# One transpose instruction per slab instead of two, in a kernel that rotates images

## Chip, cores, metric

The kernel runs on one core of a Trainium2 chip. The metric is device time in microseconds (us).

## The reference

```python
x = np.random.randn(32, 3, 256, 256).astype(np.float32)

def reference(x):
    return np.rot90(x, k=-1, axes=(-2, -1)).astype(np.float32)
```

It is a rotation of 96 planes by 90 degrees. Nothing is computed: 25.17 MB are read, 25.17 MB are written.

## The kernel before

The input is cut into 24 slabs of 1 MB. In a slab, each of 128 partitions holds 8 rows of 256 numbers. A load brings the slab in (issued on the SyncE queue), VectorE transposes it, and a store takes it out (issued on the ScalarE queue).

```python
R = 8
n_slabs = B * C * G // P            # 24
PARTS = 2
SHORT = 2
CP = R // PARTS
# ... cut: the views ld_v and st_v, 128 partitions x 2048 numbers per slab
in_pool = ctx.enter_context(tc.tile_pool(name="in_pool", bufs=12))
out_pool = ctx.enter_context(tc.tile_pool(name="out_pool", bufs=12))

for n in range(n_slabs):
    t_in = in_pool.tile([P, R * W], fp32, tag="t_in")
    nc.sync.dma_start(out=t_in, in_=ld_v[n])

    t_out = out_pool.tile([P, R * W], fp32, tag="t_out")
    src = t_in.rearrange("p (r g c) -> p c r g", r=R, c=R)
    dst = t_out.rearrange("p (c g r) -> p c r g", c=R, r=R)[:, :, ::-1, ::-1]
    for k in range(PARTS):
        cs = slice(k * CP, (k + 1) * CP)
        nc.vector.transpose(out=dst[:, cs], in_=src[:, cs])

    nc.scalar.dma_start(out=st_v[n], in_=t_out,
                        max_dma_last_dim=2048 if n < SHORT else 8192)
```

One store covers both halves of a slab, so it waits for both transposes (in the profile the second one of the first slab ends at 9.53 us and the first store is issued at 9.57 us). There are 12 buffers on each side, so loads can run far ahead.

## Time and profile before

| | before |
|---|---|
| time, median (lowest to highest) of the first 3 runs | 124.44 us (124.3 to 124.59) |
| span of the profiled run | 122.8 us |
| VectorE busy | 92.5 us, 75% |
| data moved, mean rate over the span | 50.34 MB, 410 GB/s |

The first page of the profile of the kernel before: the rows of busy tenths and of GB/s cut the span into 40 equal slices, and a 9 is 90% or more; DMA is the mean of the 16 DMA engines. The group line gives busy time, mean ns of one instruction and the idle time ahead of it.

```profile
span 122.8 us, 186 instructions
DVE 92.5 (75%) x48; POOL 0.2 (0%) x4
DVE  0199999999999999999999999897796693000000
...
DMA  3999999999999999999999999999999999999993
GB/s 93 422 427 427 393 427 422 415 420 432 426 408 411 427 427 427 427 427 427 427 427 430 427 427 427 427 427 430 427 430 427 427 427 430 424 427 427 427 430 163
...
q14 instruction: 1, 0.01, 0.0%
...
L54 DVE STREAM_TRANSPOSE t_out<-t_in 128x1024 f32<-128x1024 f32 x48 | 92.5, 2047 | 9.7 <-DMA t_in<-in_x_dram 7.9
```

The DVE row (VectorE) is full through the middle, and that alone would make VectorE look like the bound. The DMA row says more: it is full from the second slice to the last but one. So the DMA engines had transfers to work on all that time, even where VectorE was waiting or had finished.

The timeline of VectorE in the kernel before (start and duration in us; in brackets the idle time ahead and what ended it):

```profile
5.55 72.62 DVE L54 STREAM_TRANSPOSE t_out<-t_in 128x1024 f32<-128x1024 f32 x38 [5.55 <-DMA t_in<-in_x_dram]
78.62 3.98 DVE L54 STREAM_TRANSPOSE t_out<-t_in 128x1024 f32<-128x1024 f32 x2 [0.45 <-DMA t_in<-in_x_dram]
...
98.27 3.98 DVE L54 STREAM_TRANSPOSE t_out<-t_in 128x1024 f32<-128x1024 f32 x2 [0.97 <-DMA t_in<-in_x_dram]
```

VectorE is behind the loads until 78.17 us, with 38 transposes in one unbroken row. Then it has caught up and waits for each load. It ends at 98.27 + 3.98 = 102.25 us.

The windows view of the kernel before (busy time of VectorE and GpSimd, count of instructions, clock, share of the DMA engines' time, GB/s in each stretch of us):

```profile
12.00:42.00 30.00, 30.00 (x17) 0.00 (x0) 1.00 1.02 418
42.00:78.00 36.00, 36.00 (x19) 0.00 (x0) 1.00 1.01 427
78.00:102.00 24.00, 19.84 (x11) 0.00 (x0) 1.00 1.02 429
102.00:120.00 18.00, 0.25 (x1) 0.00 (x0) 1.00 1.01 425
120.00:123.00 3.00, 0.00 (x0) 0.00 (x0) 1.00 0.32 134
```

The rate is the same where VectorE is full (42 to 78 us), where it waits (78 to 102 us) and where it has nothing to do (102 to 120 us). In those last 18 us only stores move (the last packet of a load ends at 97.73 us): about seven slabs that VectorE had finished and that had been queueing, 18 us x 425 GB/s = 7.7 MB.

### The profile page before, as it was taken

What the parts mean: (1) busy time and instruction counts of PE and PEld (TensorE: products, weight loads), DVE (VectorE), ACT (ScalarE), POOL (GpSimd) and SP (SyncE); (2) the same over time, 40 slices, a digit from 0 to 9 for tenths busy, and PEclk for the clock granted to TensorE, in tenths of its full rate; (3) what the DMA queues carried; (4) which work ended last, traced back from release to release, by engine and by line L of the source; (5) the groups of instructions that cost most, each with busy time, mean ns of one, the idle gap of its engine ahead of it and who ended that gap; (6) DMA issues with size and microseconds to landing.
All of it is one profiled execution on the core that took longest, in us unless ns stands there. A gap on an engine that the chain in (4) does not pass through costs nothing.

```text
span 122.8 us, 186 instructions
## 1 busy us (share of the span) xinstructions
DVE 92.5 (75%) x48; POOL 0.2 (0%) x4
## 2 busy tenths in 40 slices
DVE  0199999999999999999999999897796693000000
POOL 0000000000000000000000000000000000000000
DMA  3999999999999999999999999999999999999993
GB/s 93 422 427 427 393 427 422 415 420 432 426 408 411 427 427 427 427 427 427 427 427 430 427 427 427 427 427 430 427 430 427 427 427 430 424 427 427 427 430 163
DMA packets 7681, 50.34 MB, mean 410 GB/s; under 512 B 768, under 2 KB 768, under 8 KB 1792
## 3 DMA queue, kind: packets, MB, share of 16 engines
q1 hardware_dynamic: 3456, 25.17, 49.3%
q10 hardware_dynamic: 4224, 25.17, 48.9%
q14 instruction: 1, 0.01, 0.0%
HBM read 25.17 MB, written 25.17 MB: 410 GB/s over the span
## 4 chain that ended last, share of the span: by engine, by line
DMA 72%; DVE 8%; DVEq 2%; SPq 1%; issue 0%
DMA t_in<-in_x_dram 72%; DVE t_out L54 8%; DVEq L83 2%; SPq L47 1%; DVEq L54 0%
## 5 line engine op out<-in xcount | busy, mean ns | idle before, releaser
L54 DVE STREAM_TRANSPOSE t_out<-t_in 128x1024 f32<-128x1024 f32 x48 | 92.5, 2047 | 9.7 <-DMA t_in<-in_x_dram 7.9
L72 POOL MEMSET const-bfloat16-1.0<- 128x1 bf16 x1 | 0.1, 101 | 0.0
L72 POOL MEMSET const-uint8-127<- 128x1 uint8 x1 | 0.1, 101 | 0.0
L72 POOL MEMSET const-float32-0.0<- 128x1 f32 x1 | 0.1, 98 | 0.2 <-issue 0.2
L72 POOL MEMSET const-float32-1.0<- 128x1 f32 x1 | 0.1, 98 | 0.0
## 6 DMA issues: line engine op xcount, KB each, us to landing
t_in<-in_x_dram SPq DMA_DIRECT2D x24, 1024.0 KB, 14.5
out_dram<-t_out ACTq DMA_DIRECT2D x24, 1024.0 KB, 19.5
```

The costliest lines, as they stand in the source:

```text
L47: nc.sync.dma_start(out=t_in, in_=ld_v[n])
L54: nc.vector.transpose(out=dst[:, cs], in_=src[:, cs])
L72: nc = _bacc.Bacc("TRN2", target_bir_lowering=False, num_devices=1)
L83: with _tile.TileContext(nc) as tc:
```

## The change

The intent: a slab needs only one transpose instruction, since its store waits for both halves anyway. The hope was that VectorE then pays once instead of twice for whatever an instruction costs beyond its elements; nothing had shown such a cost before the change (it came out at 0.06 us, below). The first and the last slab keep halves, where the pipeline fills and drains.

```diff
-    PARTS = 2
     SHORT = 2
-    CP = R // PARTS
 ...
-        for k in range(PARTS):
-            cs = slice(k * CP, (k + 1) * CP)
+        parts = 2 if n in (0, n_slabs - 1) else 1
+        for k in range(parts):
+            cs = slice(k * R // parts, (k + 1) * R // parts)
             nc.vector.transpose(out=dst[:, cs], in_=src[:, cs])
```

VectorE then has 26 instructions instead of 48: 22 of 2048 elements and 4 of 1024.

## The prediction

> What bounds the kernel now. The profile's first page gives a span of 122.8 us and 50.34 MB moved; the row of GB/s by slices lies at 408 to 432 from the second slice to the 39th, and the windows view gives a DMA share of 1.0 in every window from 3 us to 120 us. At 427 GB/s the bytes alone take 50.34 MB / 427 GB/s = 117.9 us; the rest of the span is about 2.5 us until the first load flows and about 2 us after the last bytes. The chain of waits that ended last is 72% DMA loads, 8% VectorE. [...] DMA bytes bind.
>
> VectorE is busy 75% (92.5 us). 38 transposes run without a break from 5.55 us to 78.17 us: 2.043 us each, started every (72.62 - 2.04) / 37 = 1.908 us, so each overlaps the next by 0.135 us. A slab costs VectorE 3.82 us, but DMA 2.1 MB / 427 GB/s = 4.9 us. From 78 us on VectorE waits for loads (gaps of 0.45 to 0.97 us per slab). Its last instruction ends at 102.25 us; DMA then still moves data at 427 GB/s until about 120.5 us, some 18 us of stores, about 7 to 8 slabs, queued behind. So the last transposes could come ten us later unseen.
>
> What the change does. It takes away 22 of 48 VectorE instructions (slabs 1 to 22 become one instruction of 2048 elements); elements, access patterns, loads, stores and buffers stay. A store already waited for both halves of its slab, and a load that takes a buffer over also waited for both, so nothing is released earlier or later by the merging itself. First and last slab are untouched. [...] Estimate from the trace: between nothing and 0.13 us is saved. I expect a duration of 3.80 to 3.95 us and a start-to-start pitch of 3.70 to 3.82 us against 3.82 now: at most 0.13 us a slab, 2.8 us of VectorE time in all, central estimate 1.3 us.
>
> On the critical path: none of it. Before 78 us VectorE is continuous, and stores come a little earlier; they join a DMA queue that is already full; after 78 us VectorE waits for loads; at the end the store backlog hides it. The first store, which ends the load-only stretch, comes from slab 0, which keeps its halves. A small reordering of loads against stores may move the rate by some tenths of a per cent (windows from 12 to 42 us run at 392 to 433 GB/s), in either direction.
>
> Predicted: 124.4 us, 80% range 123.8 to 125.0; faster by over 2% 0.02, within 2% 0.95, slower by over 2% 0.03.
>
> Right if: span 122.3 to 123.3 us; DMA share 1.0 from 3 to 120 us at about 427 GB/s; 26 transposes, busy 90 to 92.5 us; last transpose ends at 102 +- 1.5 us, idle gaps after 70 us as before or slightly longer; last 18 us stores only.
>
> Wrong if: the larger instruction runs at another pace per element (over 4.9 us it would become the bound); the first stores come later and leave DMA idle; or the changed mix of loads and stores lowers the rate of the DMA itself.

What binds the kernel follows from the bytes, 117.9 of 122.8 us at the trace's 427 GB/s. Of the saving, what rests on the trace is the range: from nothing to the measured overlap of 0.13 us a slab, 2.8 us over 22 slabs. The central 1.3 us stands as the estimate. The forecast of 124.4 us did not use it, since the prediction put none of the saving on the critical path. The lengths of about 2.5 us before the first load and about 2 us after the last bytes are what the windows view leaves at the full rate (82 GB/s from 0 to 3 us, 134 GB/s from 120 to 123 us); the single packets start at 1.74 us and end at 121.65 us.

## The result

| | before | after |
|---|---|---|
| time, median of 6 runs (lowest to highest) | 124.45 us (124.3 to 124.7) | 124.33 us (124.15 to 124.58) |
| ratio | 1 | 0.9988 (95%: 0.9973 to 1.0004) |
| span of the profiled run | 122.8 us | 122.4 us |
| VectorE busy | 92.5 us | 91.6 us |

Here and below, a ratio is the mean time of one kernel's runs over that of the other's of the same rounds, so it is not quite the ratio of the medians. No difference of 2% is seen; here the interval also includes 1.

The first page of the profile of the changed kernel, the lines that answer to those of before (the group now mixes both sizes):

```profile
span 122.4 us, 164 instructions
DVE 91.6 (75%) x26; POOL 0.2 (0%) x4
DVE  0199999999999999999999999697796793000000
...
DMA  2999999999999999999999999999999999999994
GB/s 83 426 428 428 390 428 424 422 421 426 424 428 418 428 426 420 426 428 428 426 428 428 428 428 428 428 426 426 428 428 428 426 428 428 428 428 426 428 428 193
...
L53 DVE STREAM_TRANSPOSE t_out<-t_in 128x2048 f32<-128x2048 f32 (+1 forms) x26 | 91.6, 3647 | 10.4 <-DMA t_in<-in_x_dram 10.4
```

The groups of the changed kernel, with the two sizes kept apart:

```profile
L53 DVE STREAM_TRANSPOSE t_out<-t_in 128x2048 f32<-128x2048 f32 x22 | 83.8, 3936 | 3.8 <-DMA t_in<-in_x_dram 3.8
L53 DVE STREAM_TRANSPOSE t_out<-t_in 128x1024 f32<-128x1024 f32 x4 | 8.0, 2058 | 6.6 <-DMA t_in<-in_x_dram 6.6
```

The timeline and the windows view of the changed kernel:

```profile
5.65 71.81 DVE L53 STREAM_TRANSPOSE t_out<-t_in 128x1024 f32<-128x1024 f32 x20 [5.65 <-DMA t_in<-in_x_dram]
78.46 3.96 DVE L53 STREAM_TRANSPOSE t_out<-t_in 128x2048 f32<-128x2048 f32 x1 [1.00 <-DMA t_in<-in_x_dram]
...
98.08 3.98 DVE L53 STREAM_TRANSPOSE t_out<-t_in 128x1024 f32<-128x1024 f32 x2 [0.99 <-DMA t_in<-in_x_dram]
```

```profile
42.00:78.00 36.00, 35.46 (x10) 0.00 (x0) 1.00 1.01 427
78.00:102.00 24.00, 19.76 (x6) 0.00 (x0) 1.00 1.01 428
102.00:120.00 18.00, 0.07 (x1) 0.00 (x0) 1.00 1.01 427
```

The same 19 slabs took VectorE 72.62 us in one row before and 71.81 us now, 0.8 us less (the last of them started 0.12 us later than the pitch of the others, presumably already waiting for its load). The gain did not travel further. The first wait for a load, at 78 us, grew from 0.45 to 1.00 us, which takes most of it back, and the last transpose ends at 98.08 + 3.98 = 102.06 us against 102.25 us. The idle time of VectorE went from 9.7 to 10.4 us. This is how a saving off the critical path looks in these two traces: busy time falls, from 92.5 to 91.6 us, and waiting grows by nearly as much.

The pitch of the merged instruction, start to start, can be read from the single starts in the row of 20: 16 of the 17 pitches lie at 3.755 to 3.770 us, mean 3.757 us, and the last, the one that was late, is 3.878 us. Two halves cost 2 x 1.908 = 3.816 us. One instruction fewer is worth 0.06 us. (The expectations below reckon with 3.77 us, which was worked out from the length of the whole row, late one included.)

### The profile page after: what moved, and what is told of

It reads as the page before. It is cut to its first block, busy times and chain, and to the rows that moved or that the text cites. A ratio compares the mean times of both kernels' runs of the same rounds, so it can differ in the third digit from the quotient of the medians.

```text
span 122.4 us, 164 instructions
## 1 busy us (share of the span) xinstructions
DVE 91.6 (75%) x26; POOL 0.2 (0%) x4
## 2 busy tenths in 40 slices
DMA packets 7680, 50.33 MB, mean 411 GB/s; under 512 B 768, under 2 KB 768, under 8 KB 1792
## 4 chain that ended last, share of the span: by engine, by line
DMA 78%; DVE 2%; DVEq 2%; SPq 1%; issue 0%
DMA t_in<-in_x_dram 78%; DVE t_out L53 2%; DVEq L82 2%; SPq L45 1%; DVEq L53 0%
## 5 line engine op out<-in xcount | busy, mean ns | idle before, releaser
L53 DVE STREAM_TRANSPOSE t_out<-t_in 128x2048 f32<-128x2048 f32 (+1 forms) x26 | 91.6, 3647 | 10.4 <-DMA t_in<-in_x_dram 10.4
```

## The experiments

Theory A was that the bytes set the time and VectorE is hidden. Rivals: VectorE is on the path (B); the merge saved time and a worse mix of DMA gave it back (C); the halves of the first and last slab hold the time (D). Unless it says otherwise, an edit is made to the changed kernel.

| run | edit | median us | ratio to before (95%) |
|---|---|---|---|
| e1_no_transpose | no VectorE work | 124.24 | 0.9982 (0.9962 to 1.0001) |
| e2_dense | transposes without strides | 124.24 | 0.998 (0.9961 to 0.9999) |
| e3_eighth_more | an eighth done twice | 124.35 | 0.9985 (0.997 to 1.0) |
| e4_half_more | half done twice | 149.41 | 1.1996 (1.1978 to 1.2014) |
| e5_eight_parts | eight instructions a slab | 125.33 | 1.0074 (1.0059 to 1.0088) |
| e6_all_whole | one instruction in every slab | 124.19 | 0.9981 (0.9968 to 0.9994) |
| e7_last_4x | last slab done 4 times | 124.29 | 0.9993 (0.9975 to 1.001) |
| e8_last_8x | last slab done 8 times | 136.65 | 1.098 (1.0963 to 1.0997) |
| e9_whole_short0 | e6, no short store pieces | 124.42 | 0.9991 (0.9976 to 1.0005) |
| e10_pool_240 | 240 memsets on GpSimd | 124.94 | 1.0029 (1.0011 to 1.0046) |
| e11_pool_960 | 960 memsets on GpSimd | 153.02 | 1.229 (1.2272 to 1.2307) |
| e12_pool_480 | 480 memsets on GpSimd | 126.03 | 1.0133 (1.0109 to 1.0157) |

### No VectorE work at all (e1_no_transpose)

```diff
-        t_out = out_pool.tile([P, R * W], fp32, tag="t_out")
-        # ... src, dst and the loop of transposes
-        nc.scalar.dma_start(out=st_v[n], in_=t_out,
+        nc.scalar.dma_start(out=st_v[n], in_=t_in,
```

in_pool has 24 buffers here, out_pool is gone, and the result is wrong.

> No transposes at all: each slab is stored from the tile it was loaded into (24 input buffers, wrong result on purpose). Theory A (DMA bytes bound the whole time, VectorE hidden): 123.3 to 124.6 us, within 1% of the kernel before. Rival B (VectorE, which runs without a break from 5.6 to 78 us, is on the path): clearly shorter, at most 110 us. Rival C (the merge saved time that a worse mix of DMA gave back): this run, free of VectorE, also comes out over 2 us below.

Measured: 124.24 us. From its page:

```profile
DMA  3999999999999999999999999999999999999994
GB/s 86 428 409 399 419 435 425 413 419 434 393 428 428 428 428 428 428 428 428 428 428 426 428 428 428 428 428 428 428 428 428 426 428 426 428 428 428 428 428 201
```

Taking all 91.6 us of VectorE work away moves the time by 0.2% against the kernel before, and its interval reaches 1. This is the strongest evidence against B and also against C: without any VectorE there is no merge to give anything back, and the time is the same. Within the noise it is also the floor for every change to VectorE in this kernel.

### Cheaper transposes (e2_dense)

```diff
-            nc.vector.transpose(out=dst[:, cs], in_=src[:, cs])
+            nc.vector.transpose(out=t_out[:, k * R // parts * W:(k + 1) * R // parts * W],
+                                in_=t_in[:, k * R // parts * W:(k + 1) * R // parts * W])
```

The result is wrong.

> The changed kernel, but source and destination of the transposes are contiguous (wrong result on purpose); instruction counts and sizes stay. Theory A: time within 1% of 124.4 us whatever the transposes cost. Rival B: falls with the VectorE time. For the instruction: if the pace of 1.82 ns per element comes from the strides of 32 bytes, 2048 elements should take 2.2 to 2.5 us; if it is the transpose's own pace, 3.9 us as in the changed kernel.

Measured: 124.24 us. The groups of this run:

```profile
L53 DVE STREAM_TRANSPOSE t_out<-t_in 128x2048 f32<-128x2048 f32 x22 | 50.8, 2311 | 38.5 <-DMA t_in<-in_x_dram 38.3
L53 DVE STREAM_TRANSPOSE t_out<-t_in 128x1024 f32<-128x1024 f32 x4 | 4.7, 1224 | 8.1 <-DMA t_in<-in_x_dram 8.1
```

The merged transpose fell from 3.94 to 2.31 us, and its group's waiting for loads grew from 3.8 to 38.5 us. So the strides set the pace of this transpose: one more element costs (3936 - 2058) / 1024 = 1.83 ns in the changed kernel and (2311 - 1224) / 1024 = 1.06 ns here. The 2.2 to 2.5 us of the expectation were the author's estimate, which no earlier run had shown. Which of the two strides, source or destination, costs the time was not separated.

### More VectorE work, below and above the DMA time (e3_eighth_more, e4_half_more)

```diff
             nc.vector.transpose(out=dst[:, cs], in_=src[:, cs])
+        nc.vector.transpose(out=dst[:, 0:1], in_=src[:, 0:1])    # e3; in e4 0:4
```

> The changed kernel with one more transpose of 256 elements per slab (an eighth done twice, same result): VectorE 3.77 + 0.51 = 4.28 us per slab, 12.3 us more in all, still below the 4.9 us that DMA takes per slab. Theory A: 124.4 us +- 0.6. Rival B: about 136 us. VectorE should end its run without a break about 10 to 25 us later than 77.5 us.

> The changed kernel with half of each slab transposed twice (same result): VectorE 3.77 + 1.91 = 5.68 us per slab, above the 4.9 us of DMA. Theory A: VectorE becomes the bound, 5.65 + 24 x 5.68 = 142 us until the last transpose ends, and about 6 us to the end of the run: 146 to 150 us. Rival B: 124.4 + 24 x 1.91 = 170 us.

e3 took 124.35 us, as A said. Three lines of its timeline, a slab's transpose, its repeat and the next slab's transpose:

```profile
9.95 3.92 DVE L53 STREAM_TRANSPOSE t_out<-t_in 128x2048 f32<-128x2048 f32 x1
13.90 0.67 DVE L54 STREAM_TRANSPOSE t_out<-t_in 128x256 f32<-128x256 f32 x1
14.46 3.92 DVE L53 STREAM_TRANSPOSE t_out<-t_in 128x2048 f32<-128x2048 f32 x1
```

One part of the expectation missed: a slab took 4.51 us and not 4.28 us, because the repeat started only when the slab's transpose had ended (3.95 us after its start, not 3.77 us) and itself took 0.56 us, not 0.51 us, until the next start; presumably it waits since it writes the same elements. That was not tested by a run of its own, but e4 points the same way: from 29 us on it does two slabs and then their two repeats, and there the first repeat starts before the transpose ahead of it, another slab's, has ended (36.50 against 36.66 us). The seven repeats of one slab in e8 also start one after the other's end, (27.92 - 3.96) / 6 = 3.99 us apart at 3.96 us each. At 4.51 us a slab VectorE therefore never caught up with the loads: it ran until 113.64 us and not until 87 to 102 us. That makes the point stronger, since 11.6 us more on the last transpose cost nothing. It also shows what the view of the chain that ended last cannot tell:

```profile
by line: DVE t_out L53 75.9%; DVE t_out L54 6.2%; issue 5.6%; DMA t_in<-in_x_dram 3.9%; DVEq L83 0.4%
```

By this line VectorE would be 82% of e3's span, but the chain ends where VectorE ends, at 113.64 us, and leaves out the stores after it; the time is that of the run without any VectorE work.

e4 took 149.41 us, in the range that A gave. Its last transpose ended at 142.42 us, 4.7 us before the end of the span of 147.1 us (the expectation's "about 6 us to the end of the run" was an estimate). Its rows:

```profile
DVE  0499999999999999999999999999999999999970
...
DMA  5999999999899999999999999999996076066066
GB/s 147 428 428 428 403 343 418 429 352 428 296 347 428 425 365 428 428 428 428 385 345 428 339 290 419 428 428 428 428 423 261 0 319 252 0 285 285 36 283 252
```

This is what the page looks like here when VectorE does bind: its row is full to the end, and holes open in the DMA row. One slab now needs 5.66 us of VectorE, against 2.1 MB / 427 GB/s = 4.9 us of DMA. So the bound changes hands between 4.5 and 5.7 us of VectorE per slab, and both kernels compared here are below, at 3.82 and 3.76 us.

### Smaller and larger instructions (e5_eight_parts, e6_all_whole)

```diff
-        parts = 2 if n in (0, n_slabs - 1) else 1
+        parts = 8    # e5; in e6 parts = 1
```

> Eight transposes of 256 elements for every slab. Estimate from the two traces: 0.048 us fixed per instruction and 1.816 ns per element, so 0.51 us start to start, 4.10 us per slab (0.33 us more than one instruction of 2048). Theory A: time as the changed kernel, 124.3 us +- 0.5. Rival B: 8 us longer. If an instruction's fixed cost is more than 0.048 us, the start-to-start time shows it.

> One transpose per slab for all slabs, the first and the last too. Theory A: nothing waits for a half, 124.3 us +- 0.4, no difference from the changed kernel. Rival D (the halves of the first and last slab hold the time, as the change assumes): up to 2 us longer.

e6: 124.19 us. The halves of the first and last slab hold nothing; D falls. It is the fastest correct version, 0.2% below the kernel before, and not to be told from the changed kernel, which was 0.1% below.

e5: a transpose of 256 elements started every (99.99 - 0.63) / 191 = 0.520 us (its timeline shows all 192 in one row of 99.99 us). With 3.757 us for a whole slab, one more instruction costs (8 x 0.520 - 3.757) / 7 = 0.06 us, as by the merging.

But e5 took 125.33 us: 0.9 us more than the kernel before, 1.0 us more than the changed kernel, and 0.5 us more than A allowed. VectorE ended at 105.6 us, well inside what e3 and e7 had for free, so it was not VectorE's time. What differs is the end of the DMA. The windows view of the last stretches of e5:

```profile
120.00:121.00 1.00, 0.00 (x0) 0.00 (x0) 1.00 0.70 295
121.00:122.00 1.00, 0.00 (x0) 0.00 (x0) 1.00 0.08 33
```

and of the changed kernel:

```profile
120.00:121.00 1.00, 0.00 (x0) 0.00 (x0) 1.00 0.74 311
121.00:122.00 1.00, 0.00 (x0) 0.00 (x0) 1.00 0.00 0
```

One DMA engine of 16 is a share of 1/16 = 0.06, and 427 GB/s over 16 engines is 26.7 GB/s each. With 0.08 and 33 GB/s, e5 looks in that microsecond as if about fifteen engines had finished and about one still worked off its part of the last store. Its page lists two packets in the instruction queue, that of the changed kernel none. From this came theory F, tested by e10 to e12.

### How much slack the last slab has (e7_last_4x, e8_last_8x)

```diff
             nc.vector.transpose(out=dst[:, cs], in_=src[:, cs])
+        for _ in range(3 if n == n_slabs - 1 else 0):    # e7; in e8 7
+            nc.vector.transpose(out=dst, in_=src)
```

> The changed kernel with the last slab transposed four times over (same result): its store is free 11.4 us later, at about 113.4 us. Theory A: the store before it ends at 118.6 us, so nothing changes: 124.3 us +- 0.5. Rival (the end hangs on the last transpose): 11 us longer.

> The changed kernel with the last slab transposed eight times over: its store is free 26.5 us later, at about 128.5 us, after the other stores have run out at 118.6 us. Theory A: the time grows by only the part that the queue of stores cannot hide, about 10 us plus the start of a DMA: 134 to 137 us. Rival (the end hangs on the last transpose): about 151 us.

e7: 124.29 us, though its last transpose ended at 102.07 + 11.95 = 114.0 us. e8: 136.65 us. Its rows:

```profile
DVE  0399999999999999999999977987889999999960
...
DMA  3999999999999999999999999999999999910015
GB/s 112 428 423 405 419 419 427 424 416 435 411 428 428 428 428 428 428 428 428 428 428 428 425 428 428 425 428 428 425 425 428 428 428 428 428 46 0 0 75 236
```

The DMA row runs on full to about 118 us, then stands empty until the last slab is done at 102.17 + 27.92 = 130.1 us. The last slab came 28.0 us late and the run took 12.3 us longer than the changed kernel, so about 15.7 us of lateness were hidden behind the queue of stores. (What the expectation calls the start of a DMA was not measured in e8; in the kernel before, the first load is issued at 0.73 us and its first packet starts at 1.74 us.) The prediction had read "ten us later unseen" from the trace.

### The mix of loads and stores (e9_whole_short0)

```diff
-    SHORT = 2
+    SHORT = 0
-        parts = 2 if n in (0, n_slabs - 1) else 1
+        parts = 1
```

> One transpose per slab for all slabs, and the first two stores no longer cut into pieces of 2 KB. Asks whether the mix of loads and stores between 12 and 42 us is worth anything. Theory A (bytes): 124.2 us +- 0.4, whatever the order. Rival C (the mix sets the rate): a difference of more than 1%.

Measured: 124.42 us. The order changes a lot: VectorE waits for loads from 32 us on instead of from 78 us, and one slice falls to 342 GB/s instead of 390. The time does not change, though the stores have 768 packets fewer (6912 in all instead of 7680). C has nothing left to stand on.

### What cost e5 its 0.9 us (e10_pool_240, e11_pool_960, e12_pool_480)

```diff
+    tiny = tiny_pool.tile([P, 1], fp32, tag="tiny")
 ...
             nc.vector.transpose(out=dst[:, cs], in_=src[:, cs])
+        for _ in range(10):    # e10; in e11 40, in e12 20
+            nc.gpsimd.memset(tiny, 0.0)
```

Nobody reads the tile, and nobody waits for these memsets. VectorE's instructions stay as in the changed kernel.

> The changed kernel with 240 memsets of one element per partition on the idle GpSimd, in a tile that nobody reads. Asks why eight transposes per slab cost 0.9 us though VectorE stayed hidden. Theory F (instructions are fetched over the DMA engines, in that trace 8 KB in 0.31 us twice, and one DMA engine that lags delays the last store): about 2 fetches more than the changed kernel's none, and 124.6 to 125.5 us. Rival G (it was the number of VectorE instructions or their semaphores): 124.3 us as the changed kernel.

> The same with 960 memsets. Theory F: 7 to 9 fetches of 8 KB; if one DMA engine takes them all, 2.2 to 2.8 us of it or more, 126.5 to 129 us, and the last packets of the store queue come one after another from one engine; if the fetches are spread over the engines, under 0.5 us. Rival G: 124.3 us, whatever the fetches.

> The changed kernel with 480 memsets on GpSimd. The run with 960 overran: its memsets started 0.156 us apart and GpSimd itself ended last. 480 end at about 76 us, so the time counts again. Theory F: 4 fetches of 8 KB (near 11, 31, 51 and 71 us), all on one DMA engine; at the 0.5 us a fetch that the delay of the last packet showed with 2 and with 6 fetches (122.19 and 124.28 us against 121.21), data end at about 123.2 us and the time is 126.1 us +- 0.5. If fetches cost only their recorded 0.31 us: 125.5 us. Rival G: 124.3 us.

e10: 124.94 us, 0.6 us more than the changed kernel. e11 missed, for a dull reason: the memsets start 0.156 us apart, so 960 take 150 us, GpSimd ended last, and the 153.02 us say nothing about DMA. Its DMA part still counts, below: 8 fetches, where 7 to 9 were expected, 6 of them before the last packet of data. With 4 for 480 memsets (e12) that is one fetch of 8 KB for 120 memsets in both runs. e12 had a number that fits: 126.03 us against 126.1 us expected. From its page, and the windows view of its end:

```profile
q14 instruction: 4, 0.03, 0.1%
```

```profile
120.00:121.00 1.00, 0.00 (x0) 0.00 (x0) 1.00 0.78 328
121.00:122.00 1.00, 0.00 (x0) 0.00 (x0) 1.00 0.06 25
122.00:123.00 1.00, 0.00 (x0) 0.00 (x0) 1.00 0.06 25
```

For two whole microseconds the share is 0.06 at 25 GB/s, as of one engine of 16 that moves data while 15 are done. The single packets of the traces give, for the profiled run of each kernel:

```
kernel      instruction fetches (8 KB each)   last 8 KB packet of
            before the last data packet       the stores ends, us
e7          0                                 121.18
after       0                                 121.21
e2          0                                 121.24
e6          0                                 121.25
e1          0                                 121.32
e9          0                                 121.58
before      1                                 121.65
e3          1                                 121.43
e10         2                                 122.19
e5          2                                 122.30
e12         4                                 123.02
e11         6                                 124.28
```

With 2, 4 and 6 fetches the end moves by 0.98, 1.81 and 3.07 us against the changed kernel, 0.45 to 0.51 us each. One fetch cannot be told from none: the two kernels with one end at 121.43 and 121.65 us, and e9, with none but another order of loads and stores, at 121.58 us. In e12 the last six packets end 0.306 us apart, one behind the other; 8 KB in 0.306 us is 26.8 GB/s, one engine's part of 427 GB/s. Had the fetches been spread over 16 engines, four of them, 4 x 0.309 us / 16 = 0.08 us for each engine, would not leave one engine 1.8 us behind. The packets also show the fetch itself take a turn: in the microseconds around a fetch 16.1 to 16.3 packets of data are under way on average (records of packets that follow each other overlap a little), and during the 309 ns of each of the 16 fetches of these runs 15.2 to 15.6. So the instruction fetches ride on the data's DMA engines, and, as the tail suggests, mostly on the same one (a packet's engine is not recorded). For e12 rival G falls, since it has the VectorE instructions of the changed kernel. For e5 itself more instructions and more fetches come together; that the fetches did it rests on its two fetches, on the same tail (its last five 8 KB packets also end 0.306 us apart) and on the size. What stays open: each fetch is recorded with 0.309 us but delays the end by about one and a half times that. Nor was it tested that GpSimd's own activity has no part; e5, with none, lies close to the same line at 0.55 us a fetch.

## Why the prediction was right

- "DMA bytes bind": shown as far as VectorE goes. Without VectorE the time is 124.24 us (e1), with 2.31 us transposes 124.24 us (e2). No run changed the number of bytes; that it is bytes rests on the steady 427 GB/s, at which they take 117.9 of the 122.8 us.
- "On the critical path: none of it": shown on both sides. The time stays with 4.51 us per slab of VectorE (e3), and goes to 149.41 us with 5.66 us (e4).
- Duration 3.80 to 3.95 us, pitch 3.70 to 3.82 us, central saving of 1.3 us in all: measured 3.94 us, 3.76 us, and about 22 x 0.06 = 1.3 us.
- The backlog of stores at the end: measured directly, about 15.7 us of slack (e7, e8).
- The point that the first slab keeps its halves, so that the first store is not late: without weight; with a whole first slab the time is 124.19 us (e6).
- The rate "in either direction" by the mix: no effect that these runs can tell (e9).
- A slip that nothing hangs on: the row of GB/s does not lie at 408 to 432 throughout, its fifth slice is at 393.
- What the prediction did not have: instruction fetches on the DMA engines. The kernel before had one in its profiled run, the changed kernel none. This could account for the 0.1 us between the medians, and for the 0.2% by which e1, e2 and e6, none of which had a fetch, lie below the kernel before. But the differences are about as large as their intervals, and e9, also without a fetch, ended its data nearly as late as the kernel before, so that is argued and not shown.

## What to carry to other kernels

A full row of an engine was not yet a bound here: VectorE worked without a break for 72.62 us, and without any of its work the time was 124.24 instead of 124.49 us (e1 and the kernel before). Look whether the DMA row is also full where that engine waits or has finished, and then try the kernel without the engine's work, which costs one wrong run and gives the floor for changes to that engine. Here the loads and stores kept the DMA engines busy to about 120 us of 122.8, and 22 saved instructions, 0.9 us of VectorE's busy time, paid 0.1 us of 124.45, within the noise. What instructions could still cost was in their fetches: the split into eight small instructions most likely lost 0.9 us that way. A late last piece was free only as long as the queue of earlier stores lasted, here about 15.7 us (e8); count that queue in your kernel.
